# Input tokens loaded into the residual's own place, and a first norm made by products with a diagonal

## The chip, the core and the metric

The kernel runs on one core of one Trainium2 chip. The metric is the device time of one execution in microseconds (us), as the median of several runs; lower is better. A core has four engines that compute, each with its own queue of instructions that it takes strictly in order: TensorE (PE in the profile; its weight loads are PEld), VectorE (DVE), ScalarE (ACT) and GpSimd (POOL). A fifth, SyncE (SP), issues the transfers (DMAs) here, also in order.

## The reference

The program is a two-layer streaming encoder for 1024 new frames and 32 frames of a running stream, in float32: layer 0 a Mamba-2 (SSD) mixer, layer 1 an HGRN2 mixer, each followed by a SwiGLU FFN. Only its beginning matters here.

```python
def rmsnorm(x, w):
    y = x * lax.rsqrt(jnp.mean(x * x, axis=-1, keepdims=True) + NORM_EPS)
    return y * w
# layer 0
h = rmsnorm(x, ssd_norm_w)                 # x: (1024 + 32, 1024)
proj = h @ ssd_in_w                        # z | x, B, C before a convolution | dt
...
x = x + out                                # the residual stream takes the mixer's output
x = x + swiglu(rmsnorm(x, ffn_norm_w))     # and so on through layer 1
```

So x is needed twice: normed, as the input of the first projection, and plain, as the residual that the mixer's output is added to much later.

## The kernel before, in words

Everything is held feature-major: a tile has 128 features as partitions and tokens along the free axis. The tokens are two halves: half 0 has 512 tokens, half 1 the other 512 and the 32 of the running stream. The residual is `acc[h][m]`, 8 tiles (m) of 128 features for each half h. A float32 product is made from three single-pass products: weights and input are each split into a high part rounded to a short float (`wh`, `xh`) and a rest (`wl`, `xl`), and PE does high x high (L303), high x rest (L304), rest x high (L305) for each of 8 blocks k of the contraction (`product`). A weight block of 512 KB is loaded by SP (L110, tile `raw`), rounded by ACT (L98) and its rest formed by DVE (L101).

The start runs as follows. `x_rows` loads x token-major, 128 tokens at a time (c = 0 to 3 in half 0), as two tiles of 512 features each (q = 0, 1). `load_x` transposes them on PE (L182, four 128x128 blocks to a PSUM bank), squares the token-major rows on ACT with a sum along the row, and copies the transposed blocks to `acc`, half of them on DVE (L189), half on ACT. `x_rstd` makes 1/rms of each token (two small DVE operations, a power on POOL). That is a column over the tokens, while the norm needs it along the free axis; `over_partitions` scales the identity by it (L202) and multiplies by a matrix of ones (L203), so that every partition has the row. `norm` then does three passes for every block of features: DVE multiplies acc by norm weight and 1/rms (L104), ACT rounds (L98), DVE takes the rest (L101). This is done for two pairs of token tiles (quarters of 256 tokens) in turn.

`ssd_layer` then takes six conv tiles for group 0 of half 0 (column blocks 16, 20, 0, 1, 2, 3 of the convolved part, in two quarters each) and, after the first, the dt projection (`ssd_dt`). Between the second and the third tile the program has the loads and transposes of half 1, and the loading and transposing of the other small vectors (`other_vectors`, `lower_bounds`). The plain transposes of half 1 are there only to fill `acc[1]` and the sums of squares; they are first read when half 0 is through. After the conv tiles come units (half, group): gate projections z (four products of 512 tokens), chunks of the scan with tasks of other products between them, a gate, and the conv tiles of the next unit (`late`).

The order in each queue is set by a scheduler that takes the program's order and priorities (`lifted`, with the norm far ahead). Transfers leave in SP's order; each takes one of eight completion semaphores in turn, so a transfer also waits for the one eight places before it. Short-lived tiles come from rings of buffers ("x", "n", "ys" and so on): a tile waits until the last reader of its predecessor in the ring is done.

Of the kernel before, what the change touches and what calls it, by code (L numbers as in the profile page):

```python
# [16 lines left out]
P = 128  # L17
# [31 lines left out]
def trunk_kernel(ctx, tc, x_prompt, x_sample, state_ssd, cache_conv, state_hgrn,  # L49
# [110 lines left out]
        scz.append(t)  # L160


    acc = [[place(LEN[h]) for m in range(KD)] for h in range(2)]

    xss = place(2 * 9).rearrange("p (a b) -> p a b", b=9)
    xr = place(9)

    def x_rows(h, c):
        src = x_sample[0] if (h, c) == (1, 4) else x_prompt[0, h * H1 + c * P:h * H1 + (c + 1) * P, :]
        n, rows = src.shape[0], []  # L170
        for q in range(2):
            rows.append(T("x", "xrow")[:n, :512])
            dma(rows[q], src[:, q * 512:(q + 1) * 512])
        return rows

    def load_x(h, c, halves=None):

        for q, rows in enumerate(halves or x_rows(h, c)):
            n = rows.shape[0]
            ps = psum_sc() if h else psum_mm()  # L180
            for j in range(4):
                PE.transpose(ps[:, j * P:j * P + n], rows[:, j * P:(j + 1) * P], ident[:n, :n])  # L182
            act(T("w", "sq")[:n, :512], rows, AF.Square, accum_out=xss[:n, q, h * 4 + c:h * 4 + c + 1])
            for j in range(4):
                dst = acc[h][q * 4 + j][:, c * P:c * P + n]
                if j % 2:
                    act(dst, ps[:, j * P:j * P + n], AF.Copy)
                else:
                    V.tensor_copy(dst, ps[:, j * P:j * P + n])  # L189

    def x_rstd(n, c0, c1):

# [135 lines left out]
    XN2 = ["x"] * 12 + ["cb"] * 4  # L328

    @lifted("norm")  # L330
    def x_norm(h, out, b0, bn):

        r = T("n", "rstd")
        for (o, n) in ((b0, min(bn, H1 - b0)), (H1, b0 + bn - H1)):
            if n > 0:
                c0, w = h * 4 + o // P, min(n, P)
                c1 = c0 + n // w
                x_rstd(w, c0, c1)
                ps = psum_sc()
                over_partitions(ps, xr[:, c0:c1], w)  # L340
                act(r[:, o - b0:o - b0 + n], ps[:, :n], AF.Copy)
        norm(h, C_SSDN, out, XN, ((b0, bn),), r)
# [28 lines left out]
    ecumd = [dp.tile([32, LEN[h]], F32, name=f"ecumd{h}") for h in range(2)]  # L371
    lastd = [dp.tile([32, 5], F32, name=f"lastd{h}") for h in range(2)]

    @lifted("dt")
    def ssd_dt(h, xn, blocks):

        L = LEN[h]
        nch = len(CHUNKS[h])
        w = wload([(q * 32, (q + 1) * 32, ssd_in_w[0][:, 5120:5152]) for q in range(4)], KD, P)
        e, v, u, ln, t = [T("ys", "dt") for _ in range(5)]  # L380
        for (b0, bn) in blocks:
            ps = psum_mm()
# [215 lines left out]
    def ssd_layer(after, w0):  # L598
# [7 lines left out]
        dts[0] = ssd_dt(0, xns[0], quarters)  # L606
        for t in ct[1:2]:
            t()
        for c in range(5):
            load_x(1, c)  # L610
        other_vectors()
        lower_bounds()
        for t in ct[2:]:
            t()
        for i, (h, g) in enumerate(units):
            u = us[i]
            tasks, late = [], []
# [3 lines left out]
            if i + 1 < len(units):  # L621
                nh, ng = units[i + 1]
                if nh != h:
                    tasks = zs + [half_two_norm] + outs + [half_two_dt]
                ct = ssd_conv_tasks(nh, ng, us[i + 1])
                tasks += ct[:EARLY]
                late = ct[EARLY:]
            else:
                tasks = zs + after[:1] + outs + after[1:]
            if g == 0:  # L630
                ssd_cols(h)
            Yt = sp.tile([P, 4 * TW], F32, tag="Y", bufs=1, name=nm("Y"))[:, :4 * LEN[1]]
# [553 lines left out]

    xns, dts = [[], []], [None, None]

    rows = [x_rows(0, c) for c in range(2)]
    first_vectors()  # L1190
    w0 = conv_w_unit(16)
    rows += [x_rows(0, c) for c in range(2, 4)]
    for q in range(2):
        for c in range(2 * q, 2 * q + 2):
            load_x(0, c, rows[c])
        x_norm(0, xns[0], q * 256, 256)
        if not q:
            w0 = wsplit(w0, KD)
    head_vectors()
# [52 lines left out]
```

## Time and profile before

| | us |
|---|---|
| time, median of 3 runs (lowest to highest) | 2893.22 (2892.77 to 2895.23) |
| the profiled execution: its own time | 2895.71 |
| its span, first to last instruction | 2894.0 |
| PE busy | 2843.8 (98%) |
| DVE, ACT busy | 2158.1 (75%), 1563.9 (54%) |

The page gives the busy time of each engine, the span in 40 slices, the transfers, the chain of work that ended last, and groups of instructions with what ended the idle time before them. From the trace come finer views: stretches ("windows", with the number of instructions in brackets, the granted clock of TensorE as a share of full speed and the share in which the transfer engines were busy), the timeline, and the list of waits. In the timeline a row is: start, duration, engine, line, operation, tiles out<-in, count, and in brackets the idle time of the engine before it with what ended that.

### The profile page before, as it was taken

How to read it: one execution, taken by the hardware profiler on the slowest of the kernel's cores; microseconds unless marked ns; L12 is line 12 of the kernel's file. 1: busy time of each engine (PE TensorE's matmuls, PEld its weight loads, DVE VectorE, ACT ScalarE, POOL GpSimd, SP SyncE). 2: the span in 40 equal slices, each digit the busy share in tenths (PEclk: the TensorE clock that was granted, in tenths of full speed). 3: DMA queues.
4: the chain of work that ended last, by engine and by line, in shares of the span. 5: the costliest groups of instructions: out<-in, count | busy, mean ns of one | idle time of the engine just before them, and what ended most of it. 6: DMA issues, size and time to landing. Idle time of an engine off the chain costs nothing. (4 is left out here: it accounts for less than half of the span.)

```text
span 2894.0 us, 49037 instructions
## 1 busy us (share of the span) xinstructions
PE 2843.8 (98%) x19655; PEld 2615.4 (90%) x19655; DVE 2158.1 (75%) x3787; ACT 1563.9 (54%) x2951; POOL 43.2 (1%) x156
## 2 busy tenths in 40 slices
PE   7999999999999999999999999999999999999998
PEld 6777888999988999999999888899988999999998
DVE  6877797777787877887777555755568877887777
ACT  6755555564643644455444655755564644554445
POOL 0000000000000000000000000000000000000000
PEclk9999999999999999999999999999999999999999
DMA  5443434444332333323333222222222332333223
GB/s 159 121 108 111 107 79 126 113 111 108 106 90 88 106 106 95 110 81 101 97 96 114 79 75 73 60 77 74 79 78 92 113 95 91 118 96 95 88 88 112
DMA packets 401343, 283.39 MB, mean 98 GB/s; under 512 B 28873, under 2 KB 386778, under 8 KB 401114
## 3 DMA queue, kind: packets, MB, share of 16 engines
q1 hardware_dynamic: 401114, 280.25, 33.3%
q8 instruction: 154, 2.52, 0.4%
q14 instruction: 75, 0.61, 0.1%
HBM read 272.39 MB, written 7.82 MB: 97 GB/s over the span
## 5 line engine op out<-in xcount | busy, mean ns | idle before, releaser
L98 ACT ACTIVATE wh<-raw 128x512 fp32r<-128x512 f32 (+1 forms) x688 | 557.1, 818 | 556.8 <-PE mm L304 431.3
L303 PE MATMUL mm<-xn,wh 128*128 128x272 f32 (+2 forms) x1552 | 524.2, 338 | 1.7 <-ACT xn L98 1.3
L304 PE MATMUL mm<-xn,wh 128*128 128x272 f32 (+2 forms) x1552 | 519.0, 335 | 1.2 <-DVE xn L101 1.2
L305 PE MATMUL mm<-xn,wl 128*128 128x272 f32 (+2 forms) x1552 | 518.0, 334 | 1.2 <-DVE wl L101 1.2
L101 DVE TENSOR_TENSOR wl<-raw,wh 128x1024 fp32r<-128x1024 f32 x308 | 375.5, 1221 | 75.4 <-ACT wh L98 57.4
L101 DVE TENSOR_TENSOR fixed<-mm,fixed 128x272 f32<-128x272 f32 (+1 forms) x512 | 262.5, 523 | 194.4 <-PE mm L305 192.8
L304 PE MATMUL mm<-fl,wh 128*128 128x272 f32 (+1 forms) x1056 | 342.3, 324 | 0.9 <-DVE fl L101 0.8
L303 PE MATMUL mm<-fh,wh 128*128 128x272 f32 (+1 forms) x1056 | 341.4, 325 | 0.6 <-DVE fixed L101 0.6
L305 PE MATMUL mm<-fh,wl 128*128 128x272 f32 (+1 forms) x1056 | 341.7, 324 | 0.0
L303 PEld LDWEIGHTS mm<-xn,wh 128*128 128x128 f32 x1552 | 292.9, 189 | 32.1 <-issue 2.8
L305 PEld LDWEIGHTS mm<-xn,wl 128*128 128x128 f32 x1552 | 292.9, 189 | 31.1 <-issue 2.0
L304 PEld LDWEIGHTS mm<-xn,wh 128*128 128x128 f32 x1552 | 292.5, 188 | 29.3 <-DVE xn L101 1.7
L101 DVE TENSOR_TENSOR wh<-raw,wh 128x512 fp32r<-128x512 f32 x380 | 256.8, 686 | 43.5 <-ACT wh L98 40.9
L940 PE MATMUL mm<-th,wh 128*128 128x272 f32 (+1 forms) x912 | 260.2, 285 | 0.1
L942 PE MATMUL mm<-th,wh 128*128 128x272 f32 (+1 forms) x912 | 259.6, 285 | 0.2 <-DVE wh L101 0.2
L941 PE MATMUL mm<-tl,wh 128*128 128x272 f32 (+1 forms) x912 | 259.6, 285 | 0.0
L304 PEld LDWEIGHTS mm<-fl,wh 128*128 128x128 f32 x1056 | 198.7, 188 | 17.2 <-DVE fl L101 2.4
L303 PEld LDWEIGHTS mm<-fh,wh 128*128 128x128 f32 x1056 | 198.3, 188 | 16.6 <-DVE fixed L101 1.0
L305 PEld LDWEIGHTS mm<-fh,wl 128*128 128x128 f32 x1056 | 198.6, 188 | 15.3
L940 PEld LDWEIGHTS mm<-th,wh 128*128 128x128 f32 x912 | 171.6, 188 | 2.0 <-ACT s L98 1.4
L941 PE MATMUL sc<-xn,wh 128*128 128x272 f32 (+1 forms) x608 | 173.1, 285 | 0.0
L942 PE MATMUL sc<-xn,wh 128*128 128x272 f32 (+1 forms) x608 | 172.8, 284 | 0.0
(247 smaller groups left out, 6628.9 us busy)
## 6 DMA issues: line engine op xcount, KB each, us to landing
raw<-in_ffn_w_down_dram SPq DMA_DIRECT2D x90, 512.0 KB, 3.5
raw<-in_ffn_w_gate_dram SPq DMA_DIRECT2D x88, 512.0 KB, 3.9
raw<-in_ffn_w_up_dram SPq DMA_DIRECT2D x88, 512.0 KB, 4.8
raw<-in_ssd_in_w_dram SPq DMA_DIRECT2D x80, 512.0 KB, 4.2
raw<-in_hgrn_in_w_dram SPq DMA_DIRECT2D x64, 512.0 KB, 4.3
cumB<-cumd SPq DMA_DIRECT2D x64, 256.0 KB, 5.0
raw<-in_ssd_out_w_dram SPq DMA_DIRECT2D x32, 512.0 KB, 3.6
raw<-in_hgrn_out_w_dram SPq DMA_DIRECT2D x16, 512.0 KB, 3.3
```

What stands on the lines that cost most here:

```text
L98: A.activation(out=out, in_=in_, func=f, **kw)
L101: (eng or V).tensor_tensor(out=out, in0=a, in1=b, op=op)
L303: PE.matmul(ps[:, :bn], a, mh, start=(k == 0), stop=False)
L304: PE.matmul(ps[:, :bn], a, ml, start=False, stop=False)
L305: PE.matmul(ps[:, :bn], b, mh, start=False, stop=(k == n - 1))
L940: PE.matmul(ps[:, :n], a, mh, start=(k == 0 and not more), stop=False, skip_group_check=True)
L941: PE.matmul(ps[:, :n], a, ml, start=False, stop=False, skip_group_check=True)
L942: PE.matmul(ps[:, :n], b, mh, start=False, stop=(k == 3), skip_group_check=True)
```

## The change

x is now loaded straight to where the residual of the same half lies. `ALL[h]` is that place as one tile of 8 x LEN[h] columns; the 1024 features of 128 tokens go, token-major, into the same 8 x 128 columns in which their transposes will stand (`x_load`). A transfer thus writes pieces of 128 numbers. Only the 32 tokens of the running stream still use tiles of the ring.

`first_norm` takes the place of transposes, ones-products and three passes: per pair of token tiles it scales the identity by 1/rms of each token (as before) and multiplies each token-major 128x128 block by that diagonal on PE (L355 of the changed kernel), which transposes and norms at once. Four such products fill a PSUM bank with two blocks of features by 256 tokens. ACT rounds from PSUM with the norm weight as its scale; one DVE operation makes the rest from PSUM. The plain transposes (`x_residual`, L194) write to the place that they read, four blocks at a time with one copy each (ACT or DVE): those of half 0 stand among the conv tiles 0 to 3 of group 0, those of half 1, with their squares, in the `late` tasks of unit 0, one token tile after each of the first conv tiles of unit 1. `other_vectors` and `lower_bounds` become tasks among the chunks of unit 0. The loads of half 1 are issued all at once after the conv tiles. `dt_weights` loads the 32 dt columns once instead of four times and repeats them by a broadcast when splitting.

Three places show how the queues move. The first is SP's queue at the start, before: x in `xrow` tiles, weights in `raw` (9 is conv tile 16; 57, four loads, is dt; 67, 109, 117, 125, 133 are conv tiles 20, 0, 1, 2, 3), and `in_ssd_D` into small columns.

```order
L110 DMA raw_57_373<-in_ssd_in_w_dram 128x8x32 x4
L110 DMA raw_67_462<-in_ssd_in_w_dram 128x8x128
L110 DMA raw_109_689<-in_ssd_in_w_dram 128x8x128
L110 DMA fixed_72<-in_ssd_dt_bias_dram 128x1x1
L110 DMA fixed_72<-in_ssd_D_dram 64x16x1 x2
L110 DMA sr_715_4300<-in_state_ssd_dram 128x4x128
L110 DMA rows_105_661<-in_ffn_norm_w_dram 16x128
...
L110 DMA raw_117_758<-in_ssd_in_w_dram 128x8x128
L110 DMA raw_125_827<-in_ssd_in_w_dram 128x8x128
L110 DMA raw_133_896<-in_ssd_in_w_dram 128x8x128
```

SP's queue at the same place now: `raw` 29 is dt, 39 and 47 are conv tiles 20 and 0, 57, 67 and 77 are conv tiles 1, 2, 3; x goes to `fixed_72`.

```order
L110 DMA raw_29_291<-in_ssd_in_w_dram 128x8x32
L110 DMA raw_39_377<-in_ssd_in_w_dram 128x8x128
L110 DMA raw_47_446<-in_ssd_in_w_dram 128x8x128
...
L110 DMA raw_57_527<-in_ssd_in_w_dram 128x8x128
...
L110 DMA raw_67_608<-in_ssd_in_w_dram 128x8x128
...
L110 DMA fixed_72<-in_ssd_D_dram 64x16x1 x2
L110 DMA fixed_72<-in_x_prompt_dram 128x4x128 x6
L110 DMA raw_77_689<-in_ssd_in_w_dram 128x8x128
L110 DMA fixed_72<-in_x_prompt_dram 128x4x128 x2
```

The weights of conv tiles 1 and 2 have moved ahead of the two loads of `in_ssd_D`; those of tile 3 stand behind them and behind six loads of half 1's x.

The second is PE's queue up to the first products, before (`mm_14` to `mm_40` are transposes of x, `sc` 203 the ones-products, `mm_53` the first product of conv tile 16):

```order
L182 MATMUL mm_36_229<-fixed_72,xrow_11_122 128x128 x4
L182 MATMUL mm_38_240<-fixed_72,xrow_12_124 128x128 x4
L182 MATMUL mm_40_251<-fixed_72,xrow_13_126 128x128 x3
L203 MATMUL sc_43_266<-fixed_72 128x128
L182 MATMUL mm_40_251<-fixed_72,xrow_13_126 128x128
L203 MATMUL sc_43_266<-fixed_72 128x128
L303 MATMUL mm_53_312<-xn_90,wh_32_214 128x256
L304 MATMUL mm_53_312<-xn_90,wh_32_214 128x256
L305 MATMUL mm_53_312<-xn_90,wl_33_215 128x256
```

PE's queue at the first products now (`sc` are banks of normed blocks, `mm_25` the first product; the three lines of `product` are L314 to L316):

```order
L355 MATMUL sc_10_133<-fixed_72 128x128 x4
L355 MATMUL sc_11_142<-fixed_72 128x128 x4
L355 MATMUL sc_12_151<-fixed_72 128x128 x4
L314 MATMUL mm_25_230<-xn_90,wh_14_169 128x256
L315 MATMUL mm_25_230<-xn_90,wh_14_169 128x256
L316 MATMUL mm_25_230<-xn_90,wl_15_170 128x256
L314 MATMUL mm_25_230<-xn_90,wh_14_169 128x256
L355 MATMUL sc_13_160<-fixed_72 128x128 x4
L315 MATMUL mm_25_230<-xn_90,wh_14_169 128x256
```

Before, all transposes of half 0 stood ahead of the first product; now three banks of diagonal products do, and the others are interleaved with products.

The third is DVE's queue at the first chunks of unit 0, before, from the copy that ends the first chunk's state:

```order
L535 COPY fixed_72<-sc_176_1152 128x512
L101 TENSOR_TENSOR fixed_72<-sc_181_1172,fixed_72 128x128
L101 TENSOR_TENSOR cumB_168_1118<-cumB_168_1118,fixed_72 128x512
L101 TENSOR_TENSOR xdt_183_1180<-sc_182_1175,fixed_72 128x512
L101 TENSOR_TENSOR xw_184_1181<-sc_182_1175,fixed_72 128x512
```

And now, from the same copy (L584):

```order
L584 COPY fixed_72<-sc_124_969 128x512
L228 COPY fixed_72<-sc_127_988 128x57
L259 TENSOR_SCALAR fixed_72<-fixed_72 128x17
L101 TENSOR_TENSOR fixed_72<-fixed_72 128x8
L228 COPY fixed_72<-sc_129_994 128x72
L101 TENSOR_TENSOR fixed_72<-fixed_72 128x8
L101 TENSOR_TENSOR fixed_72<-sc_133_1004,fixed_72 128x128
L101 TENSOR_TENSOR fixed_72<-fixed_72 128x8
L101 TENSOR_TENSOR cumB_116_935<-cumB_116_935,fixed_72 128x512
```

The small operations of `other_vectors` and `lower_bounds` now stand between the chunk's own.

The diff:

```diff
--- before.py
+++ after.py
@@ -160,33 +160,44 @@
         scz.append(t)
 
 
-    acc = [[place(LEN[h]) for m in range(KD)] for h in range(2)]
+    ALL = [place(KD * LEN[h]).rearrange("p (m t) -> p m t", m=KD) for h in range(2)]
+    acc = [[ALL[h][:, m] for m in range(KD)] for h in range(2)]
 
     xss = place(2 * 9).rearrange("p (a b) -> p a b", b=9)
     xr = place(9)
 
-    def x_rows(h, c):
-        src = x_sample[0] if (h, c) == (1, 4) else x_prompt[0, h * H1 + c * P:h * H1 + (c + 1) * P, :]
-        n, rows = src.shape[0], []
+    def x_load(h, c):
+
+        n = min(P, LEN[h] - c * P)
+        if n < P:
+            rows = [T("x", "xrow")[:n, :512].rearrange("t (m p) -> t m p", p=P) for _ in range(2)]
+            src = x_sample[0]
+        else:
+            rows = [ALL[h][:, 4 * q:4 * q + 4, c * P:(c + 1) * P] for q in range(2)]
+            src = x_prompt[0, h * H1 + c * P:h * H1 + (c + 1) * P, :]
         for q in range(2):
-            rows.append(T("x", "xrow")[:n, :512])
-            dma(rows[q], src[:, q * 512:(q + 1) * 512])
-        return rows
-
-    def load_x(h, c, halves=None):
-
-        for q, rows in enumerate(halves or x_rows(h, c)):
-            n = rows.shape[0]
-            ps = psum_sc() if h else psum_mm()
+            dma(rows[q], src[:, q * 512:(q + 1) * 512].rearrange("t (m p) -> t m p", p=P))
+        return h, c, n, rows
+
+    def x_squares(x):
+        h, c, n, rows = x
+        for q in range(2):
+            sq = T("w", "sq")[:n, :512].rearrange("t (m p) -> t m p", p=P)
+            act(sq, rows[q], AF.Square, accum_out=xss[:n, q, h * 4 + c:h * 4 + c + 1])
+
+    def x_residual(x):
+
+        h, c, n, rows = x
+        for q in range(2):
+            ps = psum_sc()
             for j in range(4):
-                PE.transpose(ps[:, j * P:j * P + n], rows[:, j * P:(j + 1) * P], ident[:n, :n])
-            act(T("w", "sq")[:n, :512], rows, AF.Square, accum_out=xss[:n, q, h * 4 + c:h * 4 + c + 1])
-            for j in range(4):
-                dst = acc[h][q * 4 + j][:, c * P:c * P + n]
-                if j % 2:
-                    act(dst, ps[:, j * P:j * P + n], AF.Copy)
-                else:
-                    V.tensor_copy(dst, ps[:, j * P:j * P + n])
+                PE.transpose(ps[:, j * P:j * P + n], rows[q][:, j], ident[:n, :n])
+            dst = ALL[h][:, 4 * q:4 * q + 4, c * P:c * P + n]
+            src = ps.rearrange("p (m t) -> p m t", m=4)[:, :, :n]
+            if q:
+                act(dst, src, AF.Copy)
+            else:
+                V.tensor_copy(dst, src)
 
     def x_rstd(n, c0, c1):
 
@@ -328,6 +339,30 @@
     XN2 = ["x"] * 12 + ["cb"] * 4
 
     @lifted("norm")
+    def first_norm(xs, out):
+
+
+        c0 = xs[0][1]
+        x_rstd(P, c0, c0 + 2)
+        ds = []
+        for c in (c0, c0 + 1):
+            ds.append(small("diag"))
+            V.tensor_scalar_mul(ds[-1], ident, xr[:, c:c + 1])
+        for m2 in range(4):
+            ps = psum_sc()
+            for j in range(4):
+                m = 2 * m2 + j // 2
+                PE.matmul(ps[:, j * P:(j + 1) * P], xs[j % 2][3][m // 4][:, m % 4], ds[j % 2],
+                          start=True, stop=True)
+            for m in (2 * m2, 2 * m2 + 1):
+                if m == len(out):
+                    out.append((XN[2 * m], XN[2 * m + 1]))
+                xh, xl = [t[:, c0 * P:(c0 + 2) * P] for t in out[m]]
+                src, w = ps[:, (m % 2) * 256:(m % 2 + 1) * 256], vc[:, C_SSDN + m:C_SSDN + m + 1]
+                act(xh, src, AF.Copy, scale=w)
+                stt(xl, src, w, xh.bitcast(F32), MUL, SUB)
+
+    @lifted("norm")
     def x_norm(h, out, b0, bn):
 
         r = T("n", "rstd")
@@ -371,12 +406,26 @@
     ecumd = [dp.tile([32, LEN[h]], F32, name=f"ecumd{h}") for h in range(2)]
     lastd = [dp.tile([32, 5], F32, name=f"lastd{h}") for h in range(2)]
 
+    @lifted("wl")
+    def dt_weights():
+
+        raw = wp.tile([P, 2 * TW], F32, tag="raw", bufs=3, name=nm("raw"))[:, :1024][:, :KD * 32]
+        raw = raw.rearrange("p (k c) -> p k c", k=KD)
+        dma(raw, ssd_in_w[0][:, 5120:5152].rearrange("(k p) c -> p k c", p=P))
+        four = raw.unsqueeze(2).to_broadcast([P, KD, 4, 32])
+        wh = wp.tile([P, 2 * TW], F32R, tag="ws", bufs=6, name=nm("wh"))[:, :1024]
+        wl = wp.tile([P, 2 * TW], F32R, tag="ws", bufs=6, name=nm("wl"))[:, :1024]
+        h4, l4 = [t.rearrange("p (k q c) -> p k q c", k=KD, q=4) for t in (wh, wl)]
+        act(h4, four, AF.Copy)
+        tt(l4, four, h4.bitcast(F32), SUB)
+        return (wh.rearrange("p (k c) -> p k c", k=KD), wl.rearrange("p (k c) -> p k c", k=KD))
+
     @lifted("dt")
     def ssd_dt(h, xn, blocks):
 
         L = LEN[h]
         nch = len(CHUNKS[h])
-        w = wload([(q * 32, (q + 1) * 32, ssd_in_w[0][:, 5120:5152]) for q in range(4)], KD, P)
+        w = dt_weights()
         e, v, u, ln, t = [T("ys", "dt") for _ in range(5)]
         for (b0, bn) in blocks:
             ps = psum_mm()
@@ -606,12 +655,8 @@
         dts[0] = ssd_dt(0, xns[0], quarters)
         for t in ct[1:2]:
             t()
-        for c in range(5):
-            load_x(1, c)
-        other_vectors()
-        lower_bounds()
-        for t in ct[2:]:
-            t()
+        run(mixed(ct[2:], [lambda x=x: x_residual(x) for x in xs]))
+        ys = [x_load(1, c) for c in range(5)]
         for i, (h, g) in enumerate(units):
             u = us[i]
             tasks, late = [], []
@@ -627,6 +672,10 @@
                 late = ct[EARLY:]
             else:
                 tasks = zs + after[:1] + outs + after[1:]
+            if i == 0:
+                seconds = [lambda x=x: (x_squares(x), x_residual(x)) for x in ys]
+                tasks = tasks[:PRE] + mixed(tasks[PRE:], [other_vectors, lower_bounds])
+                late = mixed(late, seconds)
             if g == 0:
                 ssd_cols(h)
             Yt = sp.tile([P, 4 * TW], F32, tag="Y", bufs=1, name=nm("Y"))[:, :4 * LEN[1]]
@@ -1186,14 +1235,14 @@
 
     xns, dts = [[], []], [None, None]
 
-    rows = [x_rows(0, c) for c in range(2)]
+    xs = [x_load(0, c) for c in range(2)]
     first_vectors()
     w0 = conv_w_unit(16)
-    rows += [x_rows(0, c) for c in range(2, 4)]
+    xs += [x_load(0, c) for c in range(2, 4)]
     for q in range(2):
-        for c in range(2 * q, 2 * q + 2):
-            load_x(0, c, rows[c])
-        x_norm(0, xns[0], q * 256, 256)
+        for x in xs[2 * q:2 * q + 2]:
+            x_squares(x)
+        first_norm(xs[2 * q:2 * q + 2], xns[0])
         if not q:
             w0 = wsplit(w0, KD)
     head_vectors()
```

## The prediction, made before the changed kernel was run

> **What bounds the kernel now.** I read the page first. PE is the engine on the chain of work that ended last, and it is busy nearly all of the span, so a change shows in the time only through PE: work added to its queue, or idle time and slow clock taken away.
>
> ```profile
> span 2894.0 us, 49037 instructions
> PE 2843.8 (98%) x19655; PEld 2615.4 (90%) x19655; DVE 2158.1 (75%) x3787; ACT 1563.9 (54%) x2951; POOL 43.2 (1%) x156
> ```
>
> PE is idle for 50 us. The windows show where the edited part of it lies (columns: PE, PEld, DVE, ACT, POOL busy, clock, DMA share, GB/s):
>
> ```profile
> 10.00:17.20 7.20, 5.30 (x36) 4.80 (x36) 5.89 (x22) 5.56 (x22) 1.03 (x2) 1.00 1.05 231
> 24.00:28.00 4.00, 3.50 (x18) 3.10 (x17) 4.00 (x13) 2.13 (x7) 0.00 (x0) 0.72 0.05 2
> 30.00:40.00 10.00, 10.00 (x88) 10.00 (x87) 5.80 (x8) 2.95 (x6) 1.22 (x2) 1.00 0.37 99
> 40.00:50.00 10.00, 6.82 (x60) 6.61 (x58) 4.29 (x6) 7.60 (x10) 0.43 (x1) 1.00 0.94 286
> 50.00:60.00 10.00, 5.91 (x51) 5.71 (x49) 9.57 (x18) 4.54 (x11) 0.00 (x0) 0.99 0.63 187
> 60.00:62.00 2.00, 1.88 (x9) 1.88 (x10) 0.78 (x3) 2.00 (x10) 0.00 (x0) 0.50 1.05 241
> ```
>
> Besides the start, 7 us are idle between 40 and 60, and PE runs at half clock after that. The timeline gives the three places: the first product, and two stops at a transpose of half 1's x. The second of these waited for a PSUM bank, which ACT frees in its own order, behind squares that wait for x.
>
> ```profile
> 17.29 0.36 PE L303 MATMUL mm<-xn,wh 128*128 128x256 f32 x1
> 47.95 0.65 PE L182 MATMUL sc<-fixed,xrow 128*128 128x128 f32 x4 [3.18 <-DMA xrow<-in_x_prompt_dram]
> 60.12 1.11 PE L182 MATMUL sc<-fixed,xrow 128*128 128x128 f32 x4 [4.21 <-ACT fixed L98]
> ```
>
> To turn this into lost time I count L303, of which there is one in each triple of products. The rows are windows from the start, for L303 alone (length, PE busy and count, clock, DMA share, GB/s):
>
> ```profile
> 0.00:29.07 29.07, 5.63 (x17) 0.94 0.58 147
> 0.00:44.40 44.40, 17.48 (x60) 0.96 0.55 142
> 0.00:75.00 75.00, 30.25 (x103) 0.95 0.57 153
> 0.00:100.78 100.78, 45.61 (x144) 0.97 0.55 146
> ```
>
> From 29.07 to 44.40 PE did 43 triples in 15.3 us (0.357 each) and nothing else. From 44.40 to 75.00 it did 43 triples again, in 30.6 us. The 15.3 us between hold the 40 transposes of half 1 and some other small ones; the rest is loss.
>
> **Why x comes late there.** SP's transfers leave in order, and for 18 us nothing moves:
>
> ```profile
> 18.00:20.00 2.00, 1.19 (x10) 0.93 (x8) 2.00 (x8) 1.96 (x8) 0.00 (x0) 1.00 0.06 3
> 32.00:36.00 4.00, 4.00 (x37) 4.00 (x36) 2.78 (x6) 1.21 (x3) 0.24 (x2) 1.00 0.05 2
> 36.00:40.00 4.00, 4.00 (x37) 4.00 (x36) 1.02 (x2) 0.26 (x1) 0.00 (x0) 1.00 0.85 245
> 15.01 2.43 SPq L110 DMA_DIRECT2D fixed<-in_ssd_D_dram  x2
> 42.99 4.86 SPq L110 DMA_DIRECT2D xrow<-in_x_prompt_dram  x8
> fixed<-in_ssd_D_dram SPq DMA_DIRECT2D x2, 4.0 KB, 23.0
> ```
>
> The two loads of `in_ssd_D` (4 KB each, 2 x 64 x 16 pieces of one number) take 23 us to land, and what stands behind them moves only from about 36 on: weights of conv tiles 1 to 3, then x. The change doesn't touch these loads, but moves them in the queue.
>
> **The change part by part.**
>
> *Mid-stall, 44 to 75.* Removed: the transposes of half 1 no longer stand here; those of half 0, which take their place, need no transfer. Four transposes between products cost this:
>
> ```profile
> 65.18 0.28 PE L303 MATMUL mm<-xn,wh 128*128 128x256 f32 x1
> 65.30 0.60 PE L182 MATMUL sc<-fixed,xrow 128*128 128x128 f32 x4
> 65.66 0.37 PE L304 MATMUL mm<-xn,wh 128*128 128x256 f32 x1
> 65.86 0.28 PE L305 MATMUL mm<-xn,wl 128*128 128x256 f32 x1
> ```
>
> L304 would have started at 65.30 and L305 at 65.42; L305 starts at 65.86, so four transposes cost 0.44 us. Ten such groups (two of them with 32 tokens, taken alike) and 0.6 for the four transposes of vectors and dt make 5.0 us of the 15.3 useful, and the loss 10.3 us. What of it comes back depends on the weights of tiles 1 to 3. Those of tiles 1 and 2 now leave ahead of `in_ssd_D`, those of tile 3 behind. Ahead of `in_ssd_D` now go 4.6 MB (x 2, tile 16 and tiles 20, 0, 1, 2 with 0.5 each, dt 0.1) against 4.0 MB before, all moved by 18; at the 245 GB/s of the row from 36 to 40 the 0.6 MB take 2.4 us more. So the hold starts at 20.4 and with 18 us ends at 38.4. Then six x loads (1.5 MB) and tile 3's weights go, 2 MB at 245 to 286 GB/s (the windows 36 to 40 and 40 to 50): landed by 45.4 to 46.6. Rounding and rest need two passes:
>
> ```profile
> 8.40 1.06 ACT L98 ACTIVATE wh<-raw 128x1024 fp32r<-128x1024 f32 x1 [0.90 <-DMA raw<-in_ssd_in_w_dram]
> L101 DVE TENSOR_TENSOR wl<-raw,wh 128x1024 fp32r<-128x1024 f32 x308 | 375.5, 1221 | 75.4 <-ACT wh L98 57.4
> ```
>
> That is 2.3 us, so tile 3 can start by 49. PE, dense from 25.7 (below), has done dt and tiles 20 and 0 (48 triples, 17.1 us) at 42.8, the four transpose groups for two tokens' tiles after tiles 0 and 1 and tiles 1 and 2 themselves (32 triples, 11.4) at 56: 7 us in hand. I take all 10.3; bounds 0 (tile 3's weights late by as much) and 10.3.
>
> *Transposes of half 0.* Before, they ran while nothing else could. Now 32 stand among products: 8 groups x 0.44 = 3.5 us lost. Nothing hides them. The 32 diagonal products take the transposes' old place; the four ones-products of half 0 go.
>
> *The start.* The chain to 1/rms stays:
>
> ```profile
> 7.31 0.19 ACT L98 ACTIVATION_READ_ACCUMULATOR sq<-xrow 128x1 f32 x1
> 8.82 0.50 DVE L202 TENSOR_SCALAR fixed<-fixed 128x128 f32<-128x128 f32 x2 [0.93 <-POOL fixed L101]
> 9.81 0.63 ACT L98 ACTIVATE sq<-xrow 128x512 f32<-128x512 f32 x1 [0.35 <-DMA xrow<-in_x_prompt_dram]
> 12.83 0.48 DVE L104 SCALAR_TENSOR_TENSOR xf<-fixed,rstd 128x256 f32<-128x256 f32 x1
> 13.35 0.42 ACT L98 ACTIVATE xn<-xf 128x256 fp32r<-128x256 f32 x1
> 107.58 1.06 PE L530 MATMUL sc<-ca,fixed 128*128 128x128 f32 x8
> ```
>
> Writing x in 512-byte pieces may slow its transfer: by about 0.4 us for the first pair, if it goes at the weights' rate. Diagonals are then ready at 9.7. A product with a diagonal isn't in the trace; the nearest rows are L530, four plain float32 128x128 products in 1.06 us, and L182's 0.44 for four transposes. I take L530's, so three banks are done by 13. The first norm block on ACT stands behind two squares of the next token tile (9.8 + 0.4 + 2 x 0.82 = 11.8) and can run then. Walking ACT's queue with these rows (0.42 a block, 0.82 a square, 1.06 a weight split): two squares more to 13.9, three blocks, dt's split (16.4), three blocks, tile 20's split (18.7), nine blocks and one evacuation to 22.9. DVE ends 16 rests at 0.48 and the same two splits behind it at about 24; the last triple follows. Waits for a bank (three banks, each free only when both blocks in it are split) add to that; I put 16 triples at 25.7. Before, 17 triples were started at 29.07, so the gain is 3.4 us. Bounds: 5 (DVE never waits) and 0 (the two engines' queues, not the passes removed, set the pace). The dt load of a quarter's size only helps here; it is priced at nothing, hidden by the queues above, and would be worth about 1 us if transfers were the limit.
>
> *Clock.* In 24 to 28 the clock was 0.72 before, at work that was nearly dense (3.50 of 4 us). The longest gap of PE in the 7 us ahead of it was this:
>
> ```profile
> 20.07 0.39 PE L304 MATMUL mm<-xn,wh 128*128 128x256 f32 x1 [0.88 <-DVE xn L101]
> ```
>
> A phase at half clock costs half its length. Afterwards PE's start is as patchy; a phase at the end of it would fall in dense work. I take a loss of 0.8 against before, bounds 0 and 1.5.
>
> So patchy work is enough to lower the clock. The Trainium skill, "TensorE: Matmul & The Clock Gate", section "Part 1: The HAM clock gate", has half rate after an idle window of about 3.4 us and full rate after as long a busy one. It fits the half clock at 60 after 4.2 us idle, and the 0.72 here only if the window counts patchy work as idle. By it no slow phase is due after the change, and the sum would be 0.8 us better.
>
> *Unit 0's chunks.* DVE takes the vectors' small operations where it is nearly full:
>
> ```profile
> 120.00:130.00 10.00, 10.00 (x54) 7.59 (x53) 10.00 (x17) 8.76 (x24) 0.00 (x0) 1.00 0.10 26
> 132.78 0.50 PE L305 MATMUL mm<-xn,wl 128*128 128x512 f32 x1 [0.40 <-DVE wl L101]
> L101 DVE TENSOR_TENSOR fixed<-fixed 128x8 f32<-128x8 f32 x9 | 1.3, 159 | 0.0
> ```
>
> Some 14 operations at about 0.1 (issued into each other) and three copies of 0.2 are 2 us ahead of a weight split that PE waited for already. Behind that, the ten squares of half 1 (0.82 each) and five copies come onto ACT where the gate's 1/rms is made. The moved transposes of half 1 (4.4 us, as before, now here) give PE other work meanwhile. I take 1.5 us of new wait; bounds 0 and 4.
>
> *Nothing else.* The norm of half 1, the later units and both FFNs keep their order. Rest of the residual's place: same size, same reads.
>
> **Sum:** 3.4 + 10.3 - 3.5 - 0.8 - 1.5 = 7.9 us gained. From the profiled execution's 2895.7 that gives 2887.8; it stands 2.5 above the median of the runs, so the predicted median is 2893.2 - 7.9 = 2885.3.
>
> **The rivals.**
>
> 1. *The start does not shorten.* In the new order ACT's blocks wait behind squares and splits, so PE gets its last block no earlier than before (29). For it: five squares and splits stand among ACT's first blocks, and PE takes half the diagonal products behind waiting products. Against: for a block of 256 tokens DVE does one pass instead of two and a copy, and ACT one instead of one and a copy. Gain 7.9 - 3.4 = 4.5, or less with more DVE wait in the chunks: 2889.
>
> 2. *No new waits, no slow phase.* DVE's small operations fall in its gaps before 120, the clock stays up: 7.9 + 2.3, and a start at 24.5: 2881.8. For it: PE had only 0.4 us of waits in that region. Against: DVE at 10.00 of 10.
>
> 3. *Slower: the hold by `in_ssd_D`.* Tile 3's weights and then z's stand behind it and 1.5 MB of x. If the hold lasted longer with more transfers queued, tile 3 would stop PE, us for us from a landing at 54 on, with about 1.5 us of half clock. It decides when the weights land after 54 + 7.9 - 1.5 = 60, a hold of 32 us instead of 18. Then 2893 and above; at twice the hold, 36 us, 2897. For it: the hold's length is known from one case, with little queued behind. Against: the rate of these loads is a matter of their own 2048 pieces.
>
> The Trainium skill, "DMA: Bandwidth & Descriptors", section on HWDGE ordering, has one transfer split over at most 16 rings, each consumed in its own order; by that, transfers behind `in_ssd_D` would go on in the other rings. The rows from 18 to 36 show nothing moving. By that rule rival 3 could not occur; by the rows it can.
>
> **How the numbers follow.** My forecast 0.57, with its own range 2883 to 2888; rival 1 0.22; rival 2 0.16; rival 3 0.05. A change of 0.2% (5.8 us) is about what can be told from none, so below 2887.4 is faster. That takes in rival 2 and nine tenths of the forecast, with a little of rival 1: 0.70. Same: 0.25. Slower: 0.05. Range for 8 in 10: 2880.5 to 2890, from rival 2's time to a little past rival 1's.
>
> **What would show it.** Right: the first product at about 12 to 13; 16 triples by 24 to 27; no stop of PE over 1 us from 27 to the first chunk, which starts at about 86 instead of 100.8 (100.8 - 3.4 + 0.8 - 10.3 + 3.5, and 5.0 less for what is moved behind it); transfers dead from about 20 to 38; a wait of 1 to 2 us on DVE at the fourth conv tile of unit 1. Wrong: PE waits for `wh` or `wl` of conv tile 3 or of z (rival 3); 16 triples only at 29 (rival 1); a stop at a transpose of half 1 in 120 to 150; or any difference behind 400 us.

## The result: slower, and where the profile lost it

| | before | changed |
|---|---|---|
| time, median of 7 runs each (lowest to highest), us | 2893.67 (2892.77 to 2895.23) | 2902.25 (2899.14 to 2906.18) |
| ratio, 95% interval | | 1.0031 (1.0021 to 1.0041) |
| span of the profiled execution, us | 2894.0 | 2904.4 |

The forecast was 2885.3. The changed kernel is 8.6 us slower by the medians, outside the range and on the side that had 5%. The head of the page after:

```profile
span 2904.4 us, 49072 instructions
PE 2848.8 (98%) x19711; PEld 2619.9 (90%) x19711; DVE 2152.7 (74%) x3744; ACT 1559.5 (54%) x2922; POOL 46.4 (2%) x156
```

PE works 5.0 us longer and is idle for 55.6 us instead of 50.2. Windows show that this is the sum of a gain and a larger loss. First the kernel before, from 0 to 36, 36 to 84 and 84 to 420 (columns as in the prediction: PE, PEld, DVE, ACT, POOL busy, clock, DMA share, GB/s):

```profile
0.00:36.00 36.00, 23.00 (x148) 20.44 (x149) 25.89 (x87) 23.07 (x62) 3.97 (x13) 0.95 0.48 119
36.00:84.00 48.00, 40.08 (x303) 37.84 (x302) 33.07 (x80) 35.01 (x90) 3.28 (x9) 0.96 0.55 151
84.00:420.00 336.00, 333.24 (x1752) 266.14 (x1751) 269.37 (x396) 189.72 (x349) 13.74 (x44) 1.00 0.41 111
```

and the same windows of the changed kernel:

```profile
0.00:36.00 36.00, 25.99 (x197) 25.55 (x198) 21.09 (x59) 22.92 (x48) 3.18 (x13) 1.00 0.56 140
36.00:84.00 48.00, 44.17 (x307) 41.32 (x306) 29.14 (x43) 24.70 (x46) 3.65 (x10) 0.96 0.57 147
84.00:420.00 336.00, 319.59 (x1653) 250.38 (x1652) 261.07 (x400) 185.79 (x361) 12.88 (x39) 0.99 0.38 102
```

Up to 84 PE is busy 7.1 us longer. From 84 to 420, where it had been idle for 2.8 us, it is now idle for 16.4. The prediction had nothing there but 1.5 us of one wait.

The early gain is smaller than forecast too. The changed kernel's L314 (first product of each triple) and its first chunk:

```profile
0.00:25.70 25.70, 4.58 (x15) 3.01 (x16) 1.00 0.75 194
0.00:44.40 44.40, 15.70 (x55) 10.71 (x55) 0.98 0.57 143
92.29 0.38 PE L552 MATMUL sc<-ca,ca 128*128 128x128 f32 x2
```

PE had started 15 triples by 25.7 (forecast: 16), but only 55 by 44.4 (60 before), and the first chunk came at 92.3, where 86 was forecast and 100.8 had been. Between lies a stop inside a triple that waits for no semaphore ("issue"), and a slow phase of the clock behind it. The timeline of PE, the windows around it, and SP's queue ahead of it:

```profile
38.66 0.28 PE L314 MATMUL mm<-xn,wh 128*128 128x256 f32 x1
42.77 0.28 PE L315 MATMUL mm<-xn,wh 128*128 128x256 f32 x1 [3.83 <-issue]
40.00:44.00 4.00, 1.24 (x7) 1.23 (x7) 3.97 (x8) 1.31 (x3) 0.25 (x2) 0.88 0.81 236
44.00:48.00 4.00, 4.00 (x27) 4.00 (x26) 3.64 (x6) 0.63 (x1) 0.00 (x0) 0.70 1.05 307
18.27 1.40 SPq L110 DMA_DIRECT2D fixed<-in_ssd_D_dram  x2
19.71 23.10 SPq L110 DMA_DIRECT2D fixed<-in_x_prompt_dram  x6
42.91 0.63 SPq L110 DMA_DIRECT2D raw<-in_ssd_in_w_dram  x1
```

The loss after 84 is in the waits of PE from 84 to 420, the largest of them here (total, times, longest). Before:

```profile
PE mm L305 <- DVE wl L101: 1.8, 2, 1.4
PE sc L533 <- DVE xw L101: 1.0, 1, 1.0
```

Changed:

```profile
PE sc L582 <- ACT wh L98: 5.0, 4, 1.7
PE sc L582 <- DVE xw L101: 3.3, 3, 1.4
PE mm L316 <- DVE wl L101: 3.0, 3, 2.0
```

L582 is the product of `ssd_chunk` that makes the new state from xw and the transposed B (L533 before). PE now stops there in every second of the 16 chunks, 9.3 us in all. From about 170 us to the end of this stretch PE, DVE and ACT have the same instructions in the same order as before, so the order does not explain it. What differs is what SP waits for. Each chunk loads `cumB`, the cumulative sums for eight heads, in two transfers (a pair); ACT turns them into decays in place, and the products at L593 (L544 before) read them. Waits of SP from 84 to 420, first before, then changed:

```profile
SPq L110 <- PE sc L544: 0.4, 1, 0.4
```

```profile
SPq L110 <- PE sc L593: 51.0, 15, 5.6
SPq L110 <- DVE cumB L101: 49.4, 14, 13.9
```

In the changed kernel the loads wait for the tiles that used to lie in their place: for DVE's last operation on them and then for the last products over them. Before, there was next to nothing of either. ACT, which needs the loads, stands 48.7 us for them between 84 and 420, against 2.6 before. Both sources ask for four places (`"cb": 4`), but the places are given out when the program is built. Before, pairs 3 to 6 each got other places than pairs 1 and 2, some in memory declared for other rings; now the four places serve all pairs of half 0 in turn. Pair 8, of unit 1's last chunk, shows what follows. Before (SP, ACT, PE):

```profile
177.34 1.13 SPq L110 DMA_DIRECT2D cumB<-cumd  x2
184.17 1.55 ACT L98 ACTIVATE cumB<-cumB,fixed 128x128 f32<-128x128 f32 x5
190.26 0.60 ACT L98 ACTIVATE z<-mm 128x512 f32<-128x512 f32 x1 [4.01 <-PE mm L305]
193.50 1.02 PE L533 MATMUL sc<-xw,fixed 128*128 128x512 f32 x2
```

Changed:

```profile
189.30 0.91 SPq L110 DMA_DIRECT2D cumB<-cumd  x2
193.52 1.70 ACT L98 ACTIVATE cumB<-cumB,fixed 128x128 f32<-128x128 f32 x5 [5.51 <-DMA cumB<-cumd]
195.65 0.58 ACT L98 ACTIVATE z<-mm 128x512 f32<-128x512 f32 x1
196.13 0.27 ACT L98 ACTIVATE fixed<-sc 128x128 f32<-128x128 f32 x1
197.46 0.68 DVE L101 TENSOR_TENSOR xw<-sc,fixed 128x512 f32<-128x512 f32 x1
198.29 1.10 PE L582 MATMUL sc<-xw,fixed 128*128 128x512 f32 x2 [1.16 <-ACT wh L98]
```

ACT takes its work in order. Ahead of the current chunk's gate (z) and its transposed B (`fixed`) stands the first operation on the pair for the next chunk. Before, that pair was issued 6.8 us ahead of its first use; now 4.2 us, and ACT stands 5.5 us for it. z is late, DVE's xw stands behind z's second step, and PE stops. (The product reads xw, which ends at 198.14; the bracket names `wh`, which ends at the same time.)

### The profile page after: what moved, and what is told of

Its sections match the earlier page's. It is cut to its first block, busy times and chain, and to the rows that moved or that the text cites. A ratio compares the mean times of both kernels' runs of the same rounds, so it can differ in the third digit from the quotient of the medians.

```text
span 2904.4 us, 49072 instructions
## 1 busy us (share of the span) xinstructions
PE 2848.8 (98%) x19711; PEld 2619.9 (90%) x19711; DVE 2152.7 (74%) x3744; ACT 1559.5 (54%) x2922; POOL 46.4 (2%) x156
## 3 DMA queue, kind: packets, MB, share of 16 engines
q1 hardware_dynamic: 401018, 279.47, 33.2%
## 5 line engine op out<-in xcount | busy, mean ns | idle before, releaser
L314 PE MATMUL mm<-xn,wh 128*128 128x272 f32 (+2 forms) x1552 | 524.8, 338 | 0.3 <-ACT wh L98 0.3
L316 PE MATMUL mm<-xn,wl 128*128 128x272 f32 (+2 forms) x1552 | 518.5, 334 | 3.2 <-DVE wl L101 3.2
L314 PE MATMUL mm<-fh,wh 128*128 128x272 f32 (+1 forms) x1056 | 341.7, 325 | 1.1 <-DVE fixed L101 0.8
L316 PE MATMUL mm<-fh,wl 128*128 128x272 f32 (+1 forms) x1056 | 341.7, 324 | 0.0
L316 PEld LDWEIGHTS mm<-xn,wl 128*128 128x128 f32 x1552 | 293.0, 189 | 37.3 <-issue 6.0
L314 PEld LDWEIGHTS mm<-xn,wh 128*128 128x128 f32 x1552 | 293.0, 189 | 29.5 <-issue 2.6
L314 PEld LDWEIGHTS mm<-fh,wh 128*128 128x128 f32 x1056 | 198.4, 188 | 17.4 <-DVE fixed L101 1.7
L316 PEld LDWEIGHTS mm<-fh,wl 128*128 128x128 f32 x1056 | 198.7, 188 | 15.3
```

The source lines that it names most:

```text
L314: PE.matmul(ps[:, :bn], a, mh, start=(k == 0), stop=False)
L316: PE.matmul(ps[:, :bn], b, mh, start=False, stop=(k == n - 1))
```

## The experiments

Two theories came out of the comparison. **Hold**: while the two loads of `in_ssd_D` (2 x 1024 single numbers) are in flight, nothing else moves, PE's own instructions included. **Places**: the loads of `cumB` wait for products because of where their tiles lie. The rival to both, **work**, is that the stops come from the copies, squares and products that the change itself put there. Each run is compared with the kernel before on the same chip (2892.6 to 2893.4 us in all three groups of runs).

### Places, in the kernel before

```
+    held, turns = [], [-1]
     def chunk_loads(h, g, c, first):
...
-            cb = T("cb", "cumB")[:, :512].rearrange("p (h t) -> p h t", t=P)
+            if not h and len(held) < 4:
+                held.append(T("cb", "cumB"))
+            turns[0] += 1
+            cb = T("cb", "cumB") if h else held[turns[0] % 4]
+            cb = cb[:, :512].rearrange("p (h t) -> p h t", t=P)
```

> The kernel before, with nothing altered but the place of cumB in half 0: four tiles are held and used in turn, so that a chunk's load waits for the last product of the chunk before the one that is running, as in the changed kernel. Theory 'places': the stops ahead of the product with xw (L539 here) appear in the kernel before as well, once a chunk at 0.8 to 1.7 us, and it gets 6 to 11 us slower: 2900 to 2905. Rival 'work': this kernel has none of the change's work in that stretch, so it stays within 2 us of 2893.7.

Measured: 2905.98 us, ratio 1.0045 (1.0031 to 1.0059); its span is 9.0 longer than the kernel before's. All engines' instructions stand in exactly the kernel before's order; only the place of `cumB` differs. The waits appear (L539 is the product with xw here):

```profile
PE sc L539 <- ACT wh L98: 4.9, 4, 1.2
PE sc L539 <- DVE xw L101: 3.6, 3, 1.6
SPq L110 <- PE sc L550: 52.5, 15, 5.7
```

So places alone cost the kernel before some 13 us (9 to 17 by the interval), a little more than expected, without any of the change's work.

### Six places in the changed kernel

```
-BUFS = {"x": 12, "ys": 8, "cb": 4, ...
+BUFS = {"x": 12, "ys": 8, "cb": 6, ...
```

> The changed kernel with one number altered: six places instead of four for the cumulative sums that each chunk loads (cumB). In the changed kernel a load of cumB is issued only 0.7 us after the last product over the tiles of the chunk before (178.02 behind the product at 177.32, 189.30 behind 188.60), because it gets the very place that this product reads; in the kernel before it was issued up to 12 us earlier. Theory 'places': this is what makes ACT wait 5.5 us for cumB with z and the transposed B queued behind, and PE wait 0.8 to 1.7 us ahead of the product with xw (L582) once a chunk, 9.3 us between 84 and 420. With six places the loads go out a chunk earlier, these waits fall to under 2 us in all, and the time to 2893 to 2896. Rival 'work': the stops come from the copies, squares and diagonal products that the change put into this stretch; then the waits stay and the time is 2900 to 2904.

Measured: 2904.4 us, ratio 1.0040 (1.0028 to 1.0053). No gain: by its own prediction, theory "places" in this simple form fails. Pair 8 in this kernel:

```profile
176.18 1.87 SPq L110 DMA_DIRECT2D cumB<-cumd  x2
179.65 1.28 ACT L98 ACTIVATE cumB<-cumB,fixed 128x128 f32<-128x128 f32 x4 [2.29 <-DMA cumB<-cumd]
182.54 0.57 ACT L98 ACTIVATE z<-mm 128x512 f32<-128x512 f32 x1
185.17 1.10 PE L582 MATMUL sc<-xw,fixed 128*128 128x512 f32 x2 [1.17 <-ACT wh L98]
```

The load does go out a chunk earlier (176.2, as before the change at 177.3). But with six places the built order has ACT's first operation on it a chunk earlier as well, and ACT meets the load 3.5 us after its issue again; between 84 and 420 it stands 36.1 us for `cumB`. What costs here is the distance between a load and the instruction that stands ready for it in an in-order queue, not the number of places.

### Places of their own for the loads

```
-            cb = T("cb", "cumB")...                  # chunk_loads
+            cb = T("cb" if h else "cd", "cumB")...   # "cd": 4
             cb3 = cums[q]                            # ssd_chunk
+            if not h:
+                cums[q] = T("cb", "cumE")...
+            src3, cb3 = cb3, cums[q]
-                act(cb3[:n, i, :n], cb3[:n, i, :n], AF.Relu, ...)
+                act(cb3[:n, i, :n], src3[:n, i, :n], AF.Relu, ...)
```

> The changed kernel, in half 0 with places of their own for what is loaded: cumB goes into four places that are free as soon as ACT has read it, and ACT's first operation (Relu) writes to another tile, the only one that the products read. Six places alone did not help: there the loads went out a chunk earlier (pair 8 at 176.18 instead of 189.30), but ACT's order moved with them, and ACT still met the load 3.5 us after its issue (179.65 after 176.18), with z and the transposed B queued behind. Theory 'ACT in order': what costs is that ACT stands at a Relu whose load was just issued. With own places the load no longer waits for the products, and ACT's Relu is held by the tile that it writes, not by the load, so ACT finds the sums there; the stops ahead of the product with xw (7 to 9 us between 84 and 420) fall to under 2 us, and the time is 2893 to 2897. Rival 'work': the stops come from the change's own work in this stretch; 2900 to 2904 then.

Measured: 2890.21 us, ratio 0.9987 (0.9978 to 0.9995), from 1.0031: a gain of 0.44% (12.7 us), and more than expected. The waits from 84 to 420, and what SP's loads wait for:

```profile
PE mm L316 <- DVE wl L101: 2.9, 2, 1.5
PE sc L585 <- DVE xw L101: 1.2, 1, 1.2
SPq L110 <- ACT cumE L98: 34.5, 18, 3.2
84.00:420.00 336.00, 331.22 (x1774) 264.88 (x1774) 273.04 (x421) 194.96 (x376) 14.41 (x43) 1.00 0.38 105
```

SP still waits, now for ACT's reading, which comes about a chunk earlier than the products; PE is idle for 4.8 us instead of 16.4, and ACT no longer stands for `cumB` at all. The change's own work is all still there, so "work" does not explain the stops. This edit also moves ACT's operations on `cumB` behind z and B in its order, so it does not by itself separate place from order. The run in the kernel before, where no instruction moved, does.

> A control: the kernel before with own places for the loads of cumB. It had no such stops (0 to 1.0 us at the product with xw), so by both theories it stays within 2 us of 2892.6; if it gets slower, own places cost something themselves, and that has to be added to what the other two runs show.

Measured: 2893.33 us, ratio 1.0000 (0.9991 to 1.0009). The control holds: the edit is worth nothing where the loads were early anyway.

### The two loads of single numbers

```
+    drow = place(32)
...
-        dv = ssd_D.rearrange("o (j q) -> q (o j)", q=2)
+        dma(drow, ssd_D[0:1, :].to_broadcast([P, 32]))
         for q in range(2):
-            dma(dcol[q * 64:(q + 1) * 64, :], dv[q:q + 1, :].to_broadcast([64, 16]))
+            G.tensor_copy(dcol[q * 64:(q + 1) * 64, :],
+                          drow[q * 64:(q + 1) * 64, :].rearrange("p (j q) -> p q j", q=2)[:, q])
```

> The changed kernel with in_ssd_D loaded as one row of 128 bytes to each partition (128 packets) and put in order by two copies of GpSimd, instead of two transfers of 1024 single values. Theory 'hold': nothing moved from 18 to 35 us while these two were in flight, x of half 1 and the next weights were issued up to 20 us late, and PE stood still for 3.8 us at 38.7 without waiting for any semaphore, while the first packet of the queue that carries instructions came at 40 to 41: its instructions were late. Then the stop goes, the clock's slow phase behind it (0.5 for some 4 us) too, and the time is 2895 to 2899. The stops once a chunk stay. Rival 'elsewhere': the packet with instructions comes when it does whatever the loads, or the gain is lost to the waits that follow: 2901 to 2904.

Measured: 2895.78 us, ratio 1.0012 (1.0004 to 1.0021): 0.19% or 5.5 us gained. The edit also lets this load leave earlier, at 8.8 us instead of 18.3, so form and place in SP's queue were changed together. The stop and the slow phase are gone and the first chunk comes at 85.7, where the prediction had put it:

```profile
36.00:44.00 8.00, 8.00 (x71) 8.00 (x71) 6.09 (x9) 4.17 (x6) 0.47 (x2) 1.00 0.03 9
85.70 0.38 PE L554 MATMUL sc<-ca,ca 128*128 128x128 f32 x2
```

The view of the transfer queues has queues of their own for instructions (packets, MB, share). In the changed kernel the window 22 to 26 has none of these, nor is there any from 10 to 38; then the window 38 to 42:

```profile
q1 hardware_dynamic: 427, 0.00, 4.7%
...
q8 instruction: 1, 0.02, 1.4%
q14 instruction: 2, 0.02, 1.2%
```

With the row, window 22 to 26:

```profile
q1 hardware_dynamic: 2431, 1.21, 104.0%
q8 instruction: 1, 0.02, 1.5%
```

The first q8 packet came some 16 us earlier, and PE did not stop. In the three kernels with the changed start and single-number loads PE stopped ("issue") for 3.8, 4.7 and 3.8 us; in the four with the row it didn't. Besides the changed kernel these are the ones with six places and with own places:

```profile
42.89 0.37 PE L315 MATMUL mm<-xn,wh 128*128 128x256 f32 x1 [4.70 <-issue]
41.07 0.37 PE L315 MATMUL mm<-xn,wh 128*128 128x256 f32 x1 [3.76 <-issue]
```

The three stops begin at different times, from 37.3 to 38.9, but at the same place of the program, behind PE's 220th matmul, and PE goes on 2.2 to 2.5 us after the first q8 packet (40.2, 40.5 and 38.8). With the row and the changed start that packet comes when PE has done 98 to 106 matmuls, a count that the changed kernel had reached by about 25 us. So that these loads, where and as they stood, cause the stop is shown; that the packet brings PE's code, and was held up for some 15 us, is inferred from the queue's name, the counts and the times.

The Trainium skill, "DMA: Bandwidth & Descriptors", section "Queues, rings and completion order", has each transfer engine take turns between the queues at packet granularity; by that an instruction packet would pass by a slow transfer of another queue after one packet. The kernel before shows one such passing, a packet of the other instruction queue in the window 26 to 30, with its loads of `in_ssd_D` in flight:

```profile
q14 instruction: 1, 0.01, 0.5%
```

The changed kernel shows none. When a packet was asked for the traces do not say, so why the first q8 packet came so late stays open.

### Both in the changed kernel, and the same edits in the kernel before

> Both edits in one kernel. If places and hold are two separate losses, their gains add: 2886 to 2891, faster than the kernel before, which is about what the prediction had forecast for the changed kernel without these two losses (2885). If one loss only uncovers the other, the time stays at 2893 to 2897.

Measured (six places and row): 2896.56 us, 1.0015 (1.0006 to 1.0024), the row's gain alone. Six places again give nothing.

> The same with in_ssd_D loaded as one row. If the two losses are separate: 2895.8 of the row alone less 7 to 9, so 2886 to 2889, faster than the kernel before. Rival: the first chunk that now comes at 85.7 instead of 100.8 only runs into weights or ACT work that is bound elsewhere, and the time stays at 2893 to 2896.

Measured (own places and row): 2887.01 us, 0.9977 (0.9968 to 0.9986). This is the fastest kernel that keeps all the work, and faster than the kernel before by 0.23%. Its first chunk comes at 87.3. The gains do not quite add: by the ratios to before, 5.5 us for the row and 12.7 for own places, 15.6 together.

> The kernel before with in_ssd_D loaded as one row, nothing else. Theory 'hold': there too nothing moved from 18 to 36, and x of half 1 and the conv weights behind it were late (PE waited 3.2 for xrow, 4.2 for ACT and went to 0.5 of its clock between 44 and 75); it gets 4 to 9 us faster, 2884 to 2889, so that the change itself (row against row) is worth nothing or less. Rival: the kernel before waits at 44 to 75 for the work on x, not for its loads, and gains 0 to 3 us: 2889 to 2893.

Measured: 2888.80 us, 0.9984 (0.9975 to 0.9993). The kernel before also gains from the row, 4.6 us. Its window from 36 to 84 and its first chunk (95.1 instead of 100.8) say where:

```profile
36.00:84.00 48.00, 45.22 (x323) 42.09 (x322) 33.18 (x80) 35.27 (x92) 3.38 (x12) 0.96 0.42 120
95.10 0.38 PE L505 MATMUL sc<-ca,ca 128*128 128x128 f32 x2
SPq L110 <- DVE xn L101: 10.4, 1, 10.4
```

The last line, from SP's waits between 12 and 48, corrects a reading of the prediction. With the row, too, next to nothing moves from 19 to 26, because SP itself stands for DVE until 26.0. So a part of the 18 dead us before the change would have been dead without the loads too. What the row does bring: x of half 1 is issued from 33.2 instead of 43.0.

> The kernel before with both edits, so that before and changed kernel stand side by side without the two losses. Own places did nothing to it (2893.3 against 2893.4) and the row took 4.6 us off: 2888 to 2890. The changed kernel with both is at 2887.0, so the change itself would be worth 1 to 3 us, against the 7.9 that the prediction summed. If it comes out at 2885 or less, the change is worth nothing even so.

Measured: 2888.43 us, 0.9985 (0.9976 to 0.9994). Side by side without the two losses, the changed kernel (2887.01) is 1.4 us faster than the kernel before by the medians and 2.3 by the ratios; the intervals overlap, so the change proper cannot be told from none.

### What the added products cost

The edit leaves the 32 plain transposes of half 0 and their copies out of the kernel with both edits; the residual of half 0 is then not the reference's.

```
-        run(mixed(ct[2:], [lambda x=x: x_residual(x) for x in xs]))
+        for t in ct[2:]:
+            t()
```

> The changed kernel with own places and the row, and without the 32 plain transposes of half 0 and their 8 copies (the residual stream of half 0 then keeps its tokens on partitions, so what is computed from it is not the reference's): the work that the diagonal products have been added to. The prediction put it at 0.44 us for each group of four on PE, 3.5 us in all, because PE never waits where they stand now. If so: 2887.0 less 3 to 4, 2883 to 2884. Rival: they stand in gaps of PE (0.7 us at ACT pre, 3.2 us at DVE wl) and cost nothing, 2886 to 2888.

Measured: 2883.14 us, 0.9967 (0.9955 to 0.9980), 3.9 us below 2887.01 by the medians and 2.9 by the ratios. The intervals overlap here too, so the times alone do not rule out the rival. The trace speaks against it: the first chunk comes 4.7 us earlier, at 82.6 instead of 87.3. The prediction's 3.5 for them fits.

## Why the prediction was wrong, by its own steps

*Nothing else.* This is the step that failed, and it cost the most: "The norm of half 1, the later units and both FFNs keep their order." From 170 us on they do, but for a few exchanges, and it does not follow that they keep their waits. A tile's place in memory is part of a program as well; after the change the build gave out the places anew, and `cumB` got places that had just been read. The prediction took the rings as the source declares them and compared orders only. Where the prediction had no loss, the runs show one of some 13 us: own places bring back 12.7 us of the changed kernel's time, and a loss of the same size appears in the kernel before when nothing but the places is altered. Why the allocation gave out the places so differently was not tried. The prediction also said that any difference behind 400 would be wrong: there was none to speak of, the loss lies from 92 to 420.

*Mid-stall, 10.3.* The transposes of half 1 no longer stop PE, as forecast, and the weights came as forecast (conv tile 3's rounded from 48.6, forecast to be usable by 49, and PE did not wait for them). But the hold took another victim. PE, denser than before, came to its 220th matmul at 38.9 while pieces of `in_ssd_D` were still moving, and stopped: 3.8 us, a slow phase at 0.70 behind it, and a first chunk at 92.3 instead of the 85.7 of the run with the row. That breaks the prediction's own sign, no stop of PE over 1 us. Rival 3 had the right place and the wrong victim: it looked at weights only, and gave the hold 5%. The hold's length was about right: 2048 pieces at some 107 a microsecond take 19 us. But the 18 dead us that it was read from were in part SP's own wait for DVE, and the "other rings" did not follow, since a transfer on at most 16 rings may be on all of them. Of the 10.3, about 4.6 could have been had without moving the transposes: they come back in the kernel before with the row alone.

*The start, 3.4.* Right: 15 triples by 25.7 against 16. The first product came at 15.5 instead of 12 to 13, without moving the end of that stretch.

*Transposes of half 0, 3.5.* In keeping with the run without them: 2.9 to 3.9, and 4.7 at the first chunk.

*Clock, 0.8.* There is one slow phase, but behind the stop, not at the patchy start. The rule of the Trainium skill, "TensorE: Matmul & The Clock Gate", section "Part 1: The HAM clock gate", half rate after an idle window of about 3.4 us, agrees with the trace here: clock 0.70 after 3.83 us idle, and 1.00 through the patchy start, where no such gap is. The 0.72 of the kernel before at 24 to 28, after gaps of 0.88 us at most in the 7 us ahead of it, stays unexplained by it. The prediction had noted that by it no slow phase was due; without the stop it was so (clock 1.00 from 0 to 84 with the row).

*Unit 0's chunks, 1.5.* Right in kind: one wait of 1.98 us for `wl` in a conv tile of unit 1, at 128. In all PE waits 3.0 us for `wl` between 84 and 420, against 1.8 before.

*The sum.* 7.9 were forecast; without hold and places the changed kernel is 1.4 to 2.3 us ahead of a kernel before that has the same two edits, which can't be told from none, and 6.4 ahead of the kernel before as it was (2893.4 to 2887.0). So the forecast's start and middle stood up to the first chunk: with the row 85.7 where 86 was forecast. Taking out the two losses that it missed brings back 15.2 of the 17.0 us between 2885.3 and 2902.25; but some 4.6 of that is to be had in the kernel before too.

## What to carry to other kernels

Where the build assigns memory, an edit early in a kernel can alter waits hundreds of instructions later without moving one of them: look for a new releaser in the list of the transfer queue's waits. An operation that stands in an in-order queue ahead of urgent work should find its data there, so judge a prefetch by the time from its issue to the instruction that first uses it, not by the count of buffers. And load a small vector as rows, then arrange it on the chip: here two 4 KB transfers in single numbers kept the transfers behind them back for some 15 us, and PE stopped while they ran.

## What was not expected of the hardware

- Two loads of 4 KB in 4-byte pieces moved at some 107 packets a microsecond (427 in 4 us) while the transfer engines were 4.7% busy, and hardly anything else moved. In the kernel before the second landed 23.0 us after its issue. In the changed kernel the profile has a landing after 13.4 us for the first and none for the second, but the small packets thin out only from 38 to 42. As one load of 128 rows of 128 bytes, `in_ssd_D` landed in 5.2 us.
- PE stopped for 3.8 to 4.7 us without any semaphore in the three kernels that reached their 220th matmul while these loads were in flight, and went on 2.2 to 2.5 us after the first packet of one instruction queue. The kernel before, in which PE had done 148 matmuls by 36 us instead of 197, did not stop so.
- A load of `cumB` (256 KB) landed 3.9 to 5.3 us after its issue in the changed kernel between 84 and 420 (median 4.5), though SP mostly needs only 1 to 2 us to issue a pair.
